# Another order of projections and attention in the three-tile halves of a ragged attention kernel, and other offsets of its code

## The chip, the cores and the metric

The kernel runs on one core of one Trainium2 chip. The metric is device time in microseconds (us) of one execution, the median of several runs; less is better. The engines are named as in the profile: PE is the matrix engine (its weight loads stand apart as PEld), ACT and DVE the two engines that read PSUM, POOL and SP the others; SP and ACT also issue DMAs. L302 is line 302 of the kernel.

## The reference, cut to what matters

For each of 32 batches only the first `seq_len` rows count (lengths between 64 and 511, the same draw each time); everything behind them is zero.

```python
x_b = x[b, :seq_len].copy()                 # seq_len x 512
qkv = np.matmul(x_b, w_qkv)                 # 512 x 1536 weights
q, k, v = np.split(qkv, 3, axis=-1)         # then 8 heads of 64
scores = scale * np.matmul(q, k.transpose(0, 2, 1))
attn = np.exp(scores - scores_max)
attn = attn / (np.sum(attn, axis=-1, keepdims=True) + 1e-08)
out_b = np.matmul(attn, v).transpose(1, 0, 2).reshape(seq_len, dim)
output[b, :seq_len] = out_b
```

## The kernel before, in words

**Pairs and halves.** The batches are sorted by length and taken in 16 pairs. Each pair has a class N (its longer length rounded up to 32, or 340), and T = ceil(N/128) row tiles. A class has its own code. One pair is two halves, h = 0 and h = 1. In a half (`half`, L646) the core does the attention of one batch and, mixed in with it, the projections (Q, K, V from x and the weights) of the next batch, g, whose width is W: N, or the next class's N in the last half of a class. With this draw the pairs are: two with T = 4, six with T = 3 (N = 384, 352, 352, 340, 320, 288), six with T = 2, two with T = 1. The change is about T = 3, the twelve halves in the middle of the run.

**The order is written by hand.** `ORDER[3]` and `DENSE` (L637, L640) are strings of tokens, and `half` turns each token into instructions on PE, ACT and DVE, in that order on each engine. `DENSE` is used where 3N fits in 1024 columns (N = 340, 320, 288), `ORDER[3]` for 384 and 352. The digit i is a pair of heads (0 to 3) or a row tile of V.

- `S` (L304): one key tile's scores for a head pair, two matmuls of N columns on the two halves of PE's rows, then one exp on ACT of 2N columns. Two slots of PSUM, s0 and s1, take turns. A half has twelve.
- `D` (L348): three key tiles at once, eight matmuls into s0 and s1 together, and two exps on ACT of 3N columns. It waits until both slots have been emptied by the exps of the `D` before (L350, L351). A half has four, for head pairs 1, 2, 3 of its own batch and pair 0 of the next one.
- `Q`, `K` (capital letter: emptied from PSUM by DVE, L408; small letter: by ACT, L407): one projection, four matmuls of W columns. `V` (L507): one row tile of V, four matmuls of 512 columns, emptied by DVE (L431).
- `E` then `F`, `G`, `H` or `I` of the same digit, and `U` then `W`: two projections "crossed" (L440, L453). The first token computes with the upper or lower half of the rows, the second finishes with the other half, so that two matmuls always run side by side. The second token waits for the last matmuls of the first (L455). F, G, H, I say which engines empty the Q and the K: DVE/DVE, DVE/ACT, ACT/DVE, ACT/ACT. `W` empties two V tiles by DVE.
- `A` (L511): the weighted sums of one head pair, 18 matmuls of 65 columns, then DVE normalises: a reciprocal (L574) and multiplications into `onat` (L593, L595), two in a half h = 0 and three in a half h = 1. The multiplication of `A1` raises the semaphore `s_of[h][0]`, that of `A3` `s_of[h][1]` (L599).
- `O` (L778): ACT waits for `s_of[h][0]` (L782) and then issues the DMA that stores the first half of the output columns (L1247). As every token, it has a place in ACT's queue: what stands behind it waits with it.

**Banks.** In these halves four PSUM banks (a0, a1, v0, v1) go round (`pick`, L681): a token takes the one that was given back first, or with `~` the second; PE waits until it has been emptied (L278).

**Where the code lies.** For PE the code of a class is cut (`graph`, L1102; `cut`, L70). The block `first` holds the beginning of half 0, up to the last projection that ends within `PIECE` instruction slots. It ends in a branch to `again` (the rest of half 0 and half 1, then back to `first`) if the next pair is of the same class, or to `last` (the same, then on to the next class). `align` (L1116) puts a block at an offset within units of `FETCH` = 256 instructions: `first` at `FIRST[3]`, `again` and with it `last` at `AGAIN`, for dense classes `AT_DENSE`. At the end of a pair that leaves its class PE runs one or two compares, and, where the next class follows at once, a hint and a jump (L1166, L1170, L1121); inside half 0 there is only the branch at the end of `first` (L1207).

## Time and profile before

| | us |
|---|---|
| median of 3 runs | 344.45 (343.46 to 346.18) |
| the profiled execution | 344.15 |
| its span | 342.3 |
| PE busy | 326.2 (95% of the span) |
| ACT busy | 243.5 (71%) |
| DVE busy | 207.8 (61%) |

The span is the part between the first and the last instruction that the profile holds; 1.85 us of that execution lie around it. A row of the timeline has the start in us from the span's start, the duration, engine, line, operation, output and inputs with their shape, the count of merged instructions and, in brackets, how long the engine had been idle before and what ended that. Matmul rows overlap: a matmul's printed end is modelled and includes its way through the array, so what one costs PE is read from start to start. PEq, ACTq and DVEq are the sequencers that hand instructions to their engines.

### The profile page before, as it was taken

The page shows a single profiled execution, that of the slowest core. Times are in us where ns is not written, and L with a number is a line of the kernel's source. Part 1 is how long each engine was busy: PE and PEld are TensorE (multiplying, and loading weights), DVE is VectorE, ACT ScalarE, POOL GpSimd, SP SyncE. Part 2 cuts the span into 40 slices and gives each one's busy share as a digit, 9 for nine tenths or more (in the row PEclk, how much of TensorE's full clock was granted, in tenths as well). Part 3 has the DMA queues.
Part 4 walks back from the last instruction along what each step waited for, and adds up shares of the span by engine and source line. Part 5 has one row for each costly group of instructions (what it writes and reads, how often), then busy time and mean ns, then how long its engine had stood idle before and what let it go on. Part 6 is the DMA issues. An engine that isn't in the chain of part 4 may idle for free. (4 is left out here: it accounts for less than half of the span.)

```text
span 342.3 us, 12067 instructions
## 1 busy us (share of the span) xinstructions
PE 326.2 (95%) x4286; PEld 207.3 (61%) x4287; DVE 207.8 (61%) x548; ACT 243.5 (71%) x349; POOL 63.2 (18%) x102
## 2 busy tenths in 40 slices
PE   6999999999989999999999999999899999999992
PEld 2564554455545555656656657677677776776761
DVE  4676567666654465575556546655666666667672
ACT  4568788777768878878968878878766576566441
POOL 3634020202010110110110111011111121131241
PEclk9999999999999999999999999999999999999998
DMA  6966899666846686885986897997687666778731
GB/s 200 360 196 188 259 372 250 215 198 170 213 156 181 206 274 171 269 292 158 242 305 172 214 307 231 203 255 225 201 157 184 200 183 152 177 180 158 188 106 67
DMA packets 82276, 72.15 MB, mean 211 GB/s; under 512 B 40653, under 2 KB 63181, under 8 KB 82197
## 3 DMA queue, kind: packets, MB, share of 16 engines
q1 hardware_dynamic: 70340, 59.61, 62.9%
q10 hardware_dynamic: 11856, 11.54, 9.8%
q8 instruction: 43, 0.70, 0.9%
q14 instruction: 37, 0.29, 0.3%
HBM read 25.32 MB, written 36.70 MB: 181 GB/s over the span
## 5 line engine op out<-in xcount | busy, mean ns | idle before, releaser
L344 ACT ACTIVATE ep<-psc 128x704 f16<-128x704 f32 (+7 forms) x193 | 156.7, 863 | 57.7 <-PE psc L302 40.9
L302 PE MATMUL pa<-xT,w_r 128*128 128x224 f16 (+20 forms) x996 | 141.8, 276 | 3.0 <-PEq L57 1.7
L302 PEld LDWEIGHTS pa<-xT,w_r 128*128 128x128 f16 (+1 forms) x996 | 76.4, 97 | 38.0 <-issue 17.4
L408 DVE CAST qkT<-pa 128x512 f16<-128x512 f32 (+9 forms) x82 | 47.4, 580 | 45.8 <-PE pa L302 44.5
L302 PE MATMUL pa<-w_r,xT 128*128 128x512 f16 (+3 forms) x360 | 73.4, 348 | 1.6 <-DVE qkT L408 0.9
L302 PE MATMUL psc<-qkT 64*128 64x352 f16 (+17 forms) x702 | 69.4, 287 | 1.3 <-ACT ep L376 0.6
L302 PE MATMUL pav<-v_aug,ep 128*128 128x65 f16 x1468 | 64.2, 194 | 0.0
L302 PEld LDWEIGHTS pav<-v_aug,ep 128*128 128x128 f16 x1468 | 57.4, 98 | 9.2 <-issue 1.6
L1610 POOL CAST v_aug<-masks 128x24 f16 (+4 forms) x33 | 9.1, 276 | 249.4 <-POOLq L1239 249.4
L595 DVE SCALAR_TENSOR_TENSOR onat<-pav,masks,rcp 128x128 f32<-128x128 f32 (+2 forms) x146 | 50.8, 388 | 5.3 <-DVE rcp L574 1.8
L376 ACT ACTIVATE ep<-psc 128x960 f16<-128x960 f32 (+3 forms) x48 | 43.1, 950 | 9.8 <-PE psc L302 8.1
L431 DVE TENSOR_TENSOR v_aug<-pa,masks 128x512 f16<-128x512 f32 (+1 forms) x55 | 37.2, 681 | 18.3 <-PE pa L302 16.2
L302 PEld LDWEIGHTS psc<-qkT 64*128 64x128 f16 x702 | 27.0, 94 | 34.0 <-issue 20.8
L1605 POOL CAST x<-x_nat 128x1536 f16<-128x1536 f32 (+3 forms) x33 | 42.1, 1275 | 9.0 <-POOLq L1239 8.1
L302 PEld LDWEIGHTS pa<-w_r,xT 128*128 128x128 f16 (+1 forms) x360 | 27.3, 96 | 23.2 <-issue 5.2
L407 ACT CAST qkT<-pa 128x320 f16<-128x320 f32 (+7 forms) x70 | 31.0, 460 | 12.4 <-ACTq L57 8.9
L302 PE MATMUL pav<-xT,w_r 64*128 64x352 f16 (+10 forms) x268 | 39.4, 303 | 0.0
L302 PE MATMUL pav<-w_r,xT 64*128 64x512 f16 (+3 forms) x120 | 29.5, 367 | 0.0
L574 DVE RECIPROCAL rcp<-pav 128x8 f32<-128x8 f32 (+1 forms) x74 | 14.7, 199 | 20.3 <-PE pav L302 13.2
L302 PEld LDWEIGHTS pav<-xT,w_r 64*128 64x128 f16 (+1 forms) x268 | 20.3, 95 | 7.7 <-PE pav L302 0.8
L431 DVE TENSOR_TENSOR v_aug<-pav,masks 128x512 f16<-128x512 f32 (+1 forms) x21 | 13.9, 664 | 6.0 <-PE pav L302 5.3
L408 DVE CAST qkT<-pav 128x352 f16<-128x352 f32 (+2 forms) x12 | 6.3, 528 | 17.0 <-PE pav L302 17.0
(77 smaller groups left out, 132.9 us busy)
## 6 DMA issues: line engine op xcount, KB each, us to landing
out_dram<-zt SPq DMA_DIRECT2D x16, 768.0 KB, 5.8
x_nat<-in_x_dram SPq DMA_DIRECT2D x12, 512.0 KB
x_nat<-in_x_dram SPq DMA_DIRECT2D x5, 1024.0 KB
out_dram<-onat ACTq DMA_DIRECT2D x12, 384.0 KB, 4.7
out_dram<-onat SPq DMA_DIRECT2D x12, 384.0 KB, 4.2
x_nat<-in_x_dram SPq DMA_DIRECT2D x17, 256.0 KB, 5.8
out_dram<-onat ACTq DMA_DIRECT2D x16, 256.0 KB, 3.6
x_nat<-in_x_dram SPq DMA_DIRECT2D x4, 768.0 KB
```

The source lines that it names most:

```text
L302: return lambda e: e.matmul(o, lhsT, rhs, start=start, stop=stop)
L344: lambda e: e.activation(out=dst, in_=src, func=AF.Exp, scale=scale),
L376: lambda e, par=par, b=b: e.activation(out=ep[:, i, par, 0:3, 0:N], in_=psc_f[:, par, 0 : 3 * N].rearrange("p (t n) -> p t n", n=N), func= ...
L407: return lambda e: e.copy(out=dst, in_=src)
L408: return lambda e: e.tensor_copy(out=dst, in_=src)
L431: return lambda e: e.tensor_tensor(out=v_aug[h][:, t, lo // HD : lo // HD + n, 0:HD], in0=area[b][:, 0:w].rearrange("p (a d) -> p a d", d=HD),
L574: pr.add("dve", lambda e: e.reciprocal(out=rv, in_=den).then_inc(s_r, 1))
L595: ins = e.scalar_tensor_tensor(scalar=now[0][:, 1, t : t + 1], op0=ALU.mult, op1=ALU.mult, **ops)
L1605: e.tensor_copy(out=x16[h][:, 0:T, :], in_=x_nat[h][:, 0:T, :]).then_inc(s_xc[h], 1)
L1610: e.tensor_copy(out=v_aug[h][:, 0:T, :, HD], in_=src[:, 0, 0:T].unsqueeze(2).broadcast_to([P, T, NH]),).then_inc(s_on[h], 1)
```

## The change

The two strings for T = 3 are written anew. Every token that stands for work is still there; crossed pairs and single ones are chosen differently in the dense string, and some projections are emptied by another engine. Besides, the offsets and the length of the pieces of PE's code change for T = 3.

```diff
-FIRST = {4: 20, 3: 30, 2: 20, 1: None}
-AGAIN = 110
+FIRST = {4: 20, 3: 20, 2: 20, 1: None}
+AGAIN = 2
-AT_DENSE = 0
-PIECE = 222
+AT_DENSE = 20
+PIECE = 257
...
-        3: "U0 S S W0 S E1~ S G1 S E2~ S E0 S I2 S G0 S A0 A1 V2 k3 S S Q3 O A2 A3 S",
+        3: "k3 S S E0 E2~ S F0 S I2 S A0 A1 S U0 S S W0 E1~ S S G1 A2 Q3 O A3 S S V2",
...
-    DENSE = "k3 Q0 k0 D E2~ U0 G2 W0 D q1 A0 k1 A1 D A2 q3~ V2 D O A3"
+    DENSE = "V0 D E1 E2 H1 G2 D A0 q0 O K0~ A1 D V1~ Q3 A2 k3 D A3 V2"
```

In the string for 384 and 352 the halves now end with `S S V2` where they ended with `A2 A3 S`, and begin with the single `k3` where they began with the crossed `U0`. One projection, K0, goes from ACT to DVE. In the dense string the halves end with `A3 V2` and begin with `V0`; the crossed pairs are Q1/K1 and Q2/K2 where they were Q2/K2 and V0/V1; ACT empties four projections where it emptied six. `O` stands before `A1`; it stood behind the last `D`, two tokens of attention after `A1`.

In the code as built (two instructions to a matmul) the block `first` grows from 167 to 215 instructions for 384 and 352, and from 180 to 225 for the dense classes; `last` shrinks from 547 to 500 and from 505 to 460.

## The prediction

> **What bounds the kernel now.** I read the page first, then the busy time by stretch, then PE's waits in the stretch of T = 3, then the timeline at the places that the change moves.

> ```profile
> PE 326.2 (95%) x4286; PEld 207.3 (61%) x4287; DVE 207.8 (61%) x548; ACT 243.5 (71%) x349; POOL 63.2 (18%) x102
> ```
> ```profile
> 98.80:125.30 26.50, 24.95 (x345) 14.69 (x344) 13.70 (x39) 20.45 (x34) 3.40 (x4) 1.00 0.70 209
> 125.30:174.40 49.10, 48.27 (x690) 29.86 (x688) 28.55 (x89) 40.05 (x68) 6.80 (x8) 1.00 0.80 243
> 174.40:243.40 69.00, 67.46 (x984) 46.74 (x982) 40.55 (x129) 55.12 (x84) 10.21 (x12) 1.00 0.80 224
> ```
> ```profile
> PE pa L302 <- PEq L57: 1.9, 5, 0.5
> PE pa L302 <- DVE qkT L408: 0.9, 1, 0.9
> PE pa L302 <- issue: 0.7, 1, 0.7
> PE psc L302 <- ACT ep L376: 0.6, 2, 0.3
> PE psc L302 <- PEq L57: 0.3, 1, 0.3
> ```

> The three stretches are the pair of N = 384, the two of 352, and the three dense ones; columns are length, then busy us of PE, PEld, DVE, ACT, POOL, clock, DMA share, GB/s. PE is busy 140.7 of 144.6 us, at clock 1.00, and PE's own waits there come to 4.4 us. So PE's queue sets the end; the amount of matrix work does not change, and what can be won is waits, which the last five rows name: five starts of a pair (PEq), the entry from T = 4 (DVE), one gap inside a half (issue), the exit to T = 2 (ACT, and one PEq). ACT, 55.1 of 69 us in the dense stretch, has little slack there: it can become the bound.

> **Part 1: the start of a pair.**

> ```profile
> 121.44 1.03 PE L302 MATMUL pav<-w_r,xT 128*128 128x512 f16 x4
> 122.31 0.76 PE L302 MATMUL pa<-xT,w_r 128*128 128x352 f16 x4
> 123.00 0.47 PE L302 MATMUL psc<-qkT 64*128 64x352 f16 x4
> 123.41 0.77 PE L302 MATMUL pa<-xT,w_r 128*128 128x352 f16 x4
> 124.02 1.26 PE L302 MATMUL pav<-v_aug,ep 128*128 128x65 f16 x36
> 125.21 0.32 PE L302 MATMUL psc<-qkT 64*128 64x352 f16 x2
> 125.99 1.04 PE L302 MATMUL pa<-w_r,xT 64*128 64x512 f16 x8 [0.46 <-PEq L57]
> 126.85 0.48 PE L302 MATMUL psc<-qkT 64*128 64x352 f16 x4
> 127.15 1.04 PE L302 MATMUL pa<-w_r,xT 64*128 64x512 f16 x8
> ```

> Four score matmuls take 127.15 - 126.85 = 0.30 us, so two take 0.15; after the last `S` of the pair (125.21) PE could go on at 125.36 and goes on at 125.99. The loss is 0.63, of which the row prints 0.46. Five such starts lose 1.9 + 5 x 0.17 = 2.75 us. In that time PE's sequencer goes through the branches. After the change a `V` stands last, 122.31 - 121.44 = 0.87 us long and only eight instructions, behind two `S` (0.30). The sequencer hands them over early and branches meanwhile; the loss of 0.63 lies under 0.87. In the two dense starts only `A3` (0.55) and `V` lie ahead, and the `D` before them may start late (part 3), so I leave 0.1 each: **-2.5 us**. If the cover fails, all of it stays.

> **Part 2: the entry, the exit, the gap, the switches.**

> ```profile
> 98.51 0.68 DVE L431 TENSOR_TENSOR v_aug<-pa,masks 128x512 f16<-128x512 f32 x1
> 99.11 0.58 DVE L408 CAST qkT<-pa 128x416 f16<-128x416 f32 x1
> ```
> ```profile
> 99.83 1.04 PE L302 MATMUL pa<-w_r,xT 64*128 64x512 f16 x8 [0.89 <-DVE qkT L408]
> 111.09 0.68 PE L302 MATMUL pa<-v_aug,ep 128*128 128x65 f16 x17
> 112.44 0.19 PE L302 MATMUL pa<-v_aug,ep 128*128 128x65 f16 x1 [0.67 <-issue]
> ```
> ```profile
> 243.85 0.39 PE L302 MATMUL psc<-qkT 64*128 64x256 f16 x4 [0.32 <-ACT ep L376]
> ```

> Entry: `U0` needs a0 and a1, and a1 is emptied at 99.11 + 0.58 = 99.69, 0.14 before it starts. `k3` needs a0 alone, emptied at 98.51 + 0.68 = 99.19, so it starts near 99.33, and `E0`, which needs a1, comes a microsecond later: **-0.5**. Next late is nothing: two free slots wait for the `S`.

> Exit: the first scores of T = 2 wait for the exps of the last `D`, 0.32 before the first of them, and about as much before the next. Now `V2` stands between, there 256 columns wide, half of 0.87: **-0.4**. In that half, too, `U0` crossed a V of 512 columns with one of 256 at the wide one's pace, 2 x 0.86 (125.99 to 126.85); singly they are 0.87 + 0.43: **-0.4**.

> The gap: the row of 17 `A2` matmuls and the one after a hole of 0.67. Counted from the branch to `last`, it is matmul 72, instruction 144. The block begins at offset 110 of 256: the boundary comes after 146. So I read it as code that had not arrived. With offset 2 the boundary comes after 254, in half 1, twice as long after the branch: **-0.7**, between 0 and -0.8 (start to start).

> Switches: four projection matmuls followed by a score take 123.00 - 122.31 = 0.69, followed by `A` 124.02 - 123.41 = 0.61. A change between full and half rows costs 0.08. The string for 384 and 352 has six a half where it had four (+1.0 in six halves), but `G1` comes two scores after `E1` and no longer one, which gives about 0.1 back, as do smaller bubbles: **+0.2**, between 0 and +1. The dense string has six before and after.

> **Part 3: `O` ahead of `A1`, in six dense halves.**

> ```profile
> 182.35 0.71 PE L302 MATMUL pav<-v_aug,ep 128*128 128x65 f16 x18
> 182.99 0.61 PE L302 MATMUL psc<-qkT 64*128 64x340 f16 x8
> 183.54 0.72 PE L302 MATMUL pa<-v_aug,ep 128*128 128x65 f16 x18
> 184.09 0.74 PE L302 MATMUL pa<-xT,w_r 128*128 128x340 f16 x4
> 184.67 1.03 PE L302 MATMUL pav<-w_r,xT 128*128 128x512 f16 x4
> 185.71 0.61 PE L302 MATMUL psc<-qkT 64*128 64x340 f16 x8
> ```
> ```profile
> 183.10 0.20 DVE L574 RECIPROCAL rcp<-pav 128x6 f32<-128x6 f32 x1 [0.21 <-PE pav L302]
> 183.64 1.93 ACT L376 ACTIVATE ep<-psc 128x1020 f16<-128x1020 f32 x2 [0.29 <-PE psc L302]
> 183.67 0.34 DVE L595 SCALAR_TENSOR_TENSOR onat<-pav,masks,rcp 128x128 f32<-128x128 f32 x1
> 187.13 0.38 ACTq L1247 DMA_DIRECT2D out_dram<-onat  x1
> ```
> ```profile
> 194.78 0.18 DVE L574 RECIPROCAL rcp<-pav 128x6 f32<-128x6 f32 x1
> 195.00 0.87 DVE L595 SCALAR_TENSOR_TENSOR onat<-pav,masks,rcp 128x128 f32<-128x128 f32 x3
> ```
> ```profile
> 335.30 0.75 DVE L595 SCALAR_TENSOR_TENSOR onat<-pav,masks,rcp 128x512 f32<-128x512 f32 x1 [0.25 <-DVEq L57]
> 336.30 0.56 ACTq L789 DMA_DIRECT2D out_dram<-onat  x1
> 337.08 0.60 ACT L344 ACTIVATE ep<-psc 128x512 f16<-128x512 f32 x1 [1.55 <-ACTq L57]
> ```

> The first two fences are one half 0 of N = 340. `A1` starts at 182.35, the third `D` at 182.99, its exps run 183.64 to 185.57, and the fourth `D` starts 0.14 later, at 185.71: it is the exps that hold it, by some 0.1. So from exps to next `D` is 2.07.

> After the change ACT's queue reads: exps of the second `D`, copy of Q0, wait for `A1`'s sums, DMA, exps of the third `D`. `A1` is normalised at 183.67 + 0.34 = 184.01, 1.66 after it starts. The place where ACT waits for such a store today is T = 1: normalised at 335.30 + 0.75 = 336.05, next exp at 337.08, 1.03 later, 0.56 of it the DMA. With the DMA of T = 3 (0.38) that is 0.85; the T = 1 store also raises a second semaphore, so I take 0.8. The third exps start 1.66 + 0.8 = 2.46 after `A1` starts, 1.82 after their `D` (today 0.65), and the fourth `D` can start 1.82 + 2.07 = 3.89 after the third. Meanwhile PE has that `D` (0.55 with a switch), `V1` (0.87), `Q3` (0.58), `A2` (0.55), `k3` with a switch (0.66): 3.21. PE waits **0.68**. In a half 1 DVE multiplies three times: 194.78 to 195.87 is 1.09 where half 0 has 0.91, so the exps come 0.18 later; with narrower next projections PE has 3.14 and waits 0.95. By the same sum, with matmuls and exps in proportion to their columns, the six halves wait 0.68, 0.95, 0.67, 0.99, 0.66 and 1.42 (in the last, V, Q and K are 256 wide), 5.4 us. Today the fourth `D`s wait some 0.6 in all, the PEq row of 0.3 among them: **+4.8**. From below, the DMA alone (0.38) behind sums that had long been there would cost nothing, since 183.64 + 0.38 is still within what `V1` adds; from above, 0.85 and 1.0 instead of 0.8 makes +5.1 to +6.

> **Part 4: the crossed pairs.** Between the first two `D` lie four tokens of 8 half-row matmuls, now all W wide, where two were 512 wide. At 0.86 for 512, 340 columns take 0.57 (an estimate), four of them 2.28; with the `D` 2.73. From `D` to its exps 0.65, from exps to `D` 2.07: 2.72. For 340 it just fits; for a narrower next batch it does not: by proportion 0, 0.13, 0.05, 0.25, 0.12 and 0.32, **+0.9**. In return the waits swallow small bubbles of today's dense halves: **-0.3**. Of the emptying that goes from ACT to DVE I count nothing: DVE is busy 40.6 of 69.0 us there, and every bank comes round again more than a token later.

> **Sum.** -2.5 - 0.5 - 0.4 - 0.4 - 0.7 + 0.2 + 4.8 + 0.9 - 0.3 = +1.1 us on the profiled execution of 344.15 (span 342.3 and 1.85 around it): 345.25, taken as **345.2**. The median of the runs shown, 344.45, is 0.3 above that execution, so I forecast about 0.2% over it: no change that a measurement of this kernel can tell, which takes about 1%. What is won at the pair starts, the dense halves give back.

> **The rivals.**

> *Faster: `O` does not hold the exps.* If the sums of `A1` were there 1.2 us sooner (1.82 less today's 0.65), part 3 falls away: 345.2 - 4.8 = 340.4. Against it: the token's place in ACT's queue and the T = 1 rows. For it: I have no row of T = 3 in which ACT waits like this. Chance 0.12.

> *Slower: code arrives late in every pair.* The first pieces grow to 215 and 225 instructions from offset 20, so they end at 235 and 245 of 256, and the jump then needs the next unit at once. If a hole as at 112.44 opened at each of these six branches, it would cost 6 x 0.7 and the 0.7 credited would be lost: 345.2 + 4.9 = 350.1. It decides the matter from three of the six on (348.0). Against it: eleven pieces out of twelve run today without a hole of that kind (issue: 0.7, once), and the jump has a hint ahead of it. Chance 0.09.

> ```profile
> q8 instruction: 43, 0.70, 0.9%
> ```

> 43 packets carried 0.70 MB, 16 KB each. [...]

> *The change does not do what it says: pair starts stay.* If the sequencer hands `V2` over so late that its branches do not fit under it, the 2.5 us stay: 347.7. For it: it must first get past the late `D`. Against it: eight instructions of 0.87 us. Chance 0.10.

> **How the numbers follow.** The forecast as summed has 0.62, with a range of its own of 343.5 to 346.8 (0.7 of the gap, 1 of the switches, 1 of the store either way); 0.07 is left for what I do not see. The range for 8 in 10, 342.4 to 347.9, reaches to the case of the starts and leaves out most of the other two rivals. Faster by over 1% (below 341.0) has the first rival and little else: 0.09. Slower by over 1% (above 347.9) has the second and half of the third: 0.13. Within 1%: 0.78.

> **What would show it.** Right: no PEq row above 0.1 at the starts of T = 3; first matmul of 384 near 99.3; in each dense half ACT idle up to the third exps, about 1.8 after their `D`, and a gap on PE of 0.6 to 1.4 ahead of the fourth `D`, named ACT. Wrong: exps 0.65 after the third `D` (first rival), new gaps named issue near the branches (second), PEq rows kept (third).

## The result, and the profile after

The changed kernel takes 346.88 us (median of 6 runs, 346.75 to 347.64) against 344.44 (343.46 to 346.18): a ratio of 1.0073, with a 95% interval from 1.0047 to 1.0099. Measured once more in a later session, beside new runs of the kernel before, it was 1.0071 (1.0043 to 1.0098). So it is 0.7% slower, within the 1% that the prediction calls no change. Ratios and intervals are worked out from the undisturbed executions alone and medians and ranges from all, so that two medians need not divide to the ratio beside them. The changed kernel's profiled execution took 346.75, with a span of 344.6.

The busy time by stretch, cut at the same places of the work as the prediction's first fence (the pair of 384, the two of 352, the three dense ones), and the matmul engine's waits from the entry to the exit of T = 3:

```profile
PE 325.7 (95%) x4286; PEld 206.4 (60%) x4287; DVE 215.9 (63%) x566; ACT 238.4 (69%) x331; POOL 63.1 (18%) x102
```
```profile
99.89:125.19 25.30, 25.00 (x345) 14.73 (x345) 15.16 (x45) 20.48 (x33) 3.40 (x4) 1.00 0.83 235
125.19:173.17 47.98, 47.98 (x690) 29.43 (x689) 30.21 (x93) 39.73 (x65) 6.80 (x8) 1.00 0.79 249
173.17:245.50 72.33, 67.37 (x983) 46.24 (x981) 44.70 (x137) 50.85 (x73) 10.20 (x12) 1.00 0.76 215
```
```profile
PE psc L302 <- PEq L57: 3.1, 3, 1.3
PE psc L302 <- ACT ep L376: 2.0, 4, 0.8
PE pa L302 <- DVE v_aug L431: 0.3, 1, 0.3
```

The first pair went from 26.50 to 25.30, the second stretch from 49.10 to 47.98 and has not a single wait left (PE 47.98 of 47.98). The dense stretch went from 69.00 to 72.33. The five starts on projections (`pa`) and the hole are gone from the list; in their place stand seven waits on scores (`psc`), six of them the fourth `D`s and one the exit. Three carry the name PEq: there the sequencer passed the semaphore last, but the row ahead of it on ACT is late (below); ACT had been idle for 1.95, 2.02 and 2.07 before the third exps of these halves.

From the first matmul of T = 3 to the first projection of T = 2 it takes 146.18 (100.33 to 246.51), where it took 145.04 (99.83 to 244.88); second profiles of both kernels gave 146.26 and 145.00. The entry wait, which lies ahead of that, fell from 1.05 to 0.46 start to start. So the part that the prediction works on cost 0.55, and the medians differ by 2.4. Some 0.35 of the rest lies outside the span: 2.1 to 2.3 us of every execution of the changed kernel, 1.7 to 1.9 of the kernel before. All trials below that have both new strings show the former, all others the latter; why is open. What then remains is taken up below.

Start of the first pair of 352 in the timeline, to be held against the rows at 125.21 and 125.99 of before:

```profile
123.91 0.47 PE L302 MATMUL psc<-qkT 64*128 64x352 f16 x4
124.32 1.04 PE L302 MATMUL pav<-w_r,xT 128*128 128x512 f16 x4
125.19 0.76 PE L302 MATMUL pa<-xT,w_r 128*128 128x352 f16 x4
125.88 0.47 PE L302 MATMUL psc<-qkT 64*128 64x352 f16 x4
```

`V2` at 124.32 and `k3` at 125.19 are 0.87 apart, which is V2's own length: nothing is lost. Entry and exit:

```profile
100.33 0.82 PE L302 MATMUL pa<-xT,w_r 128*128 128x384 f16 x4 [0.30 <-DVE v_aug L431]
...
246.18 0.39 PE L302 MATMUL psc<-qkT 64*128 64x256 f16 x4 [0.24 <-ACT ep L376]
```

And the first dense half, to be held against the rows from 182.35 to 185.71 of before; ACT's and DVE's rows of the same moments follow it:

```profile
179.17 0.71 PE L302 MATMUL pav<-v_aug,ep 128*128 128x65 f16 x18
179.82 0.61 PE L302 MATMUL psc<-qkT 64*128 64x340 f16 x8
180.36 1.04 PE L302 MATMUL pav<-w_r,xT 128*128 128x512 f16 x4
...
182.36 0.74 PE L302 MATMUL pav<-xT,w_r 128*128 128x340 f16 x4
183.58 0.61 PE L302 MATMUL psc<-qkT 64*128 64x340 f16 x8 [0.48 <-ACT ep L376]
```
```profile
181.07 0.38 ACTq L1247 DMA_DIRECT2D out_dram<-onat  x1
181.50 1.93 ACT L376 ACTIVATE ep<-psc 128x1020 f16<-128x1020 f32 x2 [1.58 <-ACTq L57]
```
```profile
180.49 0.34 DVE L595 SCALAR_TENSOR_TENSOR onat<-pav,masks,rcp 128x128 f32<-128x128 f32 x1
```

`A1` starts at 179.17 and is normalised at 180.49 + 0.34 = 180.83, 1.66 later, as before. ACT then issues the store (181.07) and starts the third exps at 181.50, 1.68 after their `D` (179.82); it was 0.65. The fourth `D` comes at 183.58. `Q3` alone would have let it go at 182.36 + 0.58 = 182.94, so 0.64 is lost.

### The profile page after: what moved, and what is told of

It is laid out like the page before. It is cut to its first block, busy times and chain, and to the rows that moved or that the text cites. A ratio compares the mean times of both kernels' runs of the same rounds, so it can differ in the third digit from the quotient of the medians.

```text
span 344.6 us, 12070 instructions
## 1 busy us (share of the span) xinstructions
PE 325.7 (95%) x4286; PEld 206.4 (60%) x4287; DVE 215.9 (63%) x566; ACT 238.4 (69%) x331; POOL 63.1 (18%) x102
## 5 line engine op out<-in xcount | busy, mean ns | idle before, releaser
L344 ACT ACTIVATE ep<-psc 128x704 f16<-128x704 f32 (+7 forms) x193 | 156.8, 858 | 58.6 <-PE psc L302 40.9
L302 PE MATMUL pa<-xT,w_r 128*128 128x224 f16 (+21 forms) x972 | 133.1, 276 | 4.1 <-PEq L57 1.7
L302 PEld LDWEIGHTS pa<-xT,w_r 128*128 128x128 f16 (+1 forms) x972 | 73.6, 97 | 37.3 <-issue 14.8
L302 PE MATMUL pa<-w_r,xT 128*128 128x512 f16 (+3 forms) x360 | 72.9, 348 | 0.0
L302 PE MATMUL psc<-qkT 64*128 64x352 f16 (+17 forms) x702 | 67.0, 287 | 5.3 <-PEq L57 3.1
L408 DVE CAST qkT<-pa 128x512 f16<-128x512 f32 (+9 forms) x82 | 47.3, 578 | 35.3 <-PE pa L302 34.3
L302 PE MATMUL pav<-v_aug,ep 128*128 128x65 f16 x1414 | 62.2, 194 | 0.0
L302 PEld LDWEIGHTS pav<-v_aug,ep 128*128 128x128 f16 x1414 | 55.1, 98 | 9.7 <-issue 1.2
L376 ACT ACTIVATE ep<-psc 128x960 f16<-128x960 f32 (+3 forms) x48 | 43.1, 949 | 20.8 <-ACTq L57 13.1
L431 DVE TENSOR_TENSOR v_aug<-pa,masks 128x512 f16<-128x512 f32 (+1 forms) x61 | 41.3, 682 | 18.0 <-PE pa L302 17.4
L595 DVE SCALAR_TENSOR_TENSOR onat<-pav,masks,rcp 128x128 f32<-128x128 f32 (+2 forms) x137 | 48.2, 391 | 5.6 <-DVE rcp L574 2.1
L302 PEld LDWEIGHTS psc<-qkT 64*128 64x128 f16 x702 | 26.0, 94 | 34.9 <-issue 24.2
L302 PE MATMUL pav<-xT,w_r 64*128 64x352 f16 (+11 forms) x340 | 46.2, 300 | 0.0
L302 PEld LDWEIGHTS pa<-w_r,xT 128*128 128x128 f16 (+1 forms) x360 | 27.2, 97 | 24.2 <-issue 4.7
L407 ACT CAST qkT<-pa 128x352 f16<-128x352 f32 (+7 forms) x58 | 26.3, 458 | 12.8 <-ACTq L57 6.3
L574 DVE RECIPROCAL rcp<-pav 128x8 f32<-128x8 f32 (+1 forms) x71 | 14.1, 199 | 28.5 <-PE pav L302 18.8
L302 PEld LDWEIGHTS pav<-xT,w_r 64*128 64x128 f16 (+1 forms) x340 | 24.7, 95 | 8.6 <-issue 1.1
L408 DVE CAST qkT<-pav 128x352 f16<-128x352 f32 (+5 forms) x30 | 14.8, 501 | 16.6 <-PE pav L302 15.9
L302 PE MATMUL pav<-w_r,xT 128*128 128x512 f16 (+2 forms) x72 | 17.7, 367 | 0.0
L302 PEld LDWEIGHTS pa<-v_aug,ep 128*128 128x128 f16 x378 | 13.4, 98 | 3.7 <-issue 2.2
```

Of the source, the lines that this page charges most:

```text
L302: return lambda e: e.matmul(o, lhsT, rhs, start=start, stop=stop)
L344: lambda e: e.activation(out=dst, in_=src, func=AF.Exp, scale=scale),
L376: lambda e, par=par, b=b: e.activation(out=ep[:, i, par, 0:3, 0:N], in_=psc_f[:, par, 0 : 3 * N].rearrange("p (t n) -> p t n", n=N), func= ...
L407: return lambda e: e.copy(out=dst, in_=src)
L408: return lambda e: e.tensor_copy(out=dst, in_=src)
L431: return lambda e: e.tensor_tensor(out=v_aug[h][:, t, lo // HD : lo // HD + n, 0:HD], in0=area[b][:, 0:w].rearrange("p (a d) -> p a d", d=HD),
```

## The experiments

All twelve were timed beside fresh runs of the kernel before, whose medians were 344.76 to 345.54 in these sessions; ratios are to those. "T = 3" below is the time from its first matmul to the first projection of T = 2.

**The store behind the last D** (of the changed kernel; `-` is the changed kernel, `+` the trial):

```
-    DENSE = "V0 D E1 E2 H1 G2 D A0 q0 O K0~ A1 D V1~ Q3 A2 k3 D A3 V2"
+    DENSE = "V0 D E1 E2 H1 G2 D A0 q0 K0~ A1 D V1~ Q3 A2 k3 D O A3 V2"
```

> The changed kernel with one token of the dense string moved: O stands behind the last D again, and no longer ahead of A1. Theory (the store holds the third exps): the six waits ahead of the fourth D (0.64, 1.01, 0.67, 1.09, 0.97, 1.48 in the changed kernel, 5.9 in all) fall to about 0.1 each, the third exps start some 0.65 after their D, and the time falls by 5.3, from 346.9 to 341.6 (340.8 to 342.6), below both kernels. Rival (the wide crossed pair and the copies that went to other engines hold the fourth D, the store only happens to stand there): the waits stay within a few tenths and the time stays near 346.9. In between, near 344, both have a share.

342.70 (341.0 to 343.8), ratio 0.9917 (0.9886 to 0.9948); T = 3 took 142.85. All six fourth `D`s lose 0.1, the switch alone: the 5.9 are down to 0.6. T = 3 fell by 3.3 and not by 5.3, because smaller waits came up in other places (0.52, 0.53, 0.44 and 0.44 start to start), the two longest at a crossed token:

```profile
188.12 0.72 PE L302 MATMUL pa<-xT,w_r 64*128 64x320 f16 x8 [0.34 <-PEq L57]
```
```profile
L1074 PEldq TENSOR_LOAD <-cls x16: 297/421/1022, 47.2 to 332.5; - x16
```

The second row groups the loads of the next class into a register by the matmul engine's sequencer (shortest, median, longest in ns). One of them, 0.95 long, stands just ahead of 188.12, one of 1.02 ahead of the other. A load took between 0.30 and 1.02 here, and in two halves a long one showed at a crossed token. Why their length varies is open.

**The store early in the kernel before:**

```
-    DENSE = "k3 Q0 k0 D E2~ U0 G2 W0 D q1 A0 k1 A1 D A2 q3~ V2 D O A3"
+    DENSE = "k3 Q0 k0 D E2~ U0 G2 W0 D q1 A0 k1 O A1 D A2 q3~ V2 D A3"
```

> The kernel before with one token of the dense string moved: O ahead of A1, nothing else. Theory: the third exps wait for the normalised sums of A1 and the DMA, start 1.8 after their D as in the changed kernel, and the fourth D could start 1.82 + 2.07 = 3.89 after the third, where today 2.72 pass: a wait of about 1.2 in half 0 of N = 340 and up to 1.4 in others, some 7 in all, so 351 (349.5 to 352.5). That the wait is longer than in the changed kernel is part of the theory: between the third and fourth D the old string has one token less of half-row work. Rival (the store is harmless, the other moves of the dense string cost the time): 344.4, within 0.5.

354.03 (351.9 to 354.6), ratio 1.0232 (1.0185 to 1.0278). One token does it, in the old string as well:

```profile
183.30 0.61 PE L302 MATMUL psc<-qkT 64*128 64x340 f16 x8
...
187.06 0.61 PE L302 MATMUL psc<-qkT 64*128 64x340 f16 x8 [1.06 <-ACT ep L376]
```
```profile
184.56 0.38 ACTq L1247 DMA_DIRECT2D out_dram<-onat  x1
184.98 1.93 ACT L376 ACTIVATE ep<-psc 128x1020 f16<-128x1020 f32 x2 [1.33 <-ACTq L57]
```

The third exps start 184.98 - 183.30 = 1.68 after their `D`, as in the changed kernel, and the fourth `D` 3.76 after the third, in both. The six waits are 1.22, 1.46, 1.18, 1.53, 1.12 and 1.97, 8.5 in all, so 7.2 more than the 1.3 of before. The expectation had "some 7"; T = 3 grew by 9.3, and part of the other 2 is a lower clock behind these waits (a mean of 0.75 from 203 to 208, last section).

**The store behind the third D** (of the changed kernel):

```
+    DENSE = "V0 D E1 E2 H1 G2 D A0 q0 K0~ A1 D O V1~ Q3 A2 k3 D A3 V2"
```

> The changed kernel with O one step later in the dense string: right behind the third D (and its exps on ACT), no longer ahead of A1. Theory (what counts is only that the store stands ahead of the third exps in ACT's queue): the six waits ahead of the fourth D go as they did with O behind the last D (0.1 each, the switch), 342.7 (341.5 to 344). The sums of A1 are normalised some 1.0 after the third exps start, and these last 1.9, so ACT has nothing to wait for there. Rival (a store in the middle of the half costs its issue of 0.38 in any place): the fourth exps come 0.4 later and each half keeps 0.3 to 0.4, 345.

342.26 (340.9 to 343.5), ratio 0.9923 (0.9890 to 0.9955); T = 3 took 141.32, the shortest of all. ACT's rows of the same half:

```profile
181.08 1.02 ACT L376 ACTIVATE ep<-psc 128x1020 f16<-128x1020 f32 x1 [0.54 <-PE psc L302]
181.80 0.38 ACTq L1247 DMA_DIRECT2D out_dram<-onat  x1
182.00 1.01 ACT L376 ACTIVATE ep<-psc 128x1020 f16<-128x1020 f32 x1
```

The store is now issued at 181.80, while the first of the two exps runs, and the second follows at 182.00, 0.92 after the first; the pair elsewhere keeps that distance too (1.93 for both, of which the second takes 1.01). So the 0.38 itself cost nothing here, where the sums were ready under an exp; what cost was ACT standing still for them (1.58 idle ahead of the third exps in the changed kernel, 0.29 in the kernel before).

**The long string alone, and the dense one alone.** The first is the changed kernel with the old `DENSE`; the second is the kernel before with the new `DENSE`, `AT_DENSE = 20` and `PIECE = 257`.

> One half of the change: the new string of N = 384 and 352 and the new code places, with the old dense string. Theory (the long string gains, the dense one loses): three pair starts gone (0.64, 0.46, 0.53), the entry 0.6 shorter, the hole of 0.8 gone, four more switches and smaller bubbles for about +0.2 in all: 3 us less than the kernel before, 341.4 by its median of 344.4 (340.4 to 342.6), with the two starts between dense pairs (0.6 and 0.5) still there. Rival (the old dense string does not fit the new places, as the old long string did not): a jump of 2 us or more at one of the dense starts, 345 or more.

> The other half of the change: the new dense string at its new place (20, pieces up to 257), with the old string of N = 384 and 352 at its old places (30 and 110). Theory: the stretch of the dense pairs takes 73.4 instead of 69.7 us, as in the changed kernel, the rest as before: 348.1 (347 to 349), and with the part of the long string (3 less) it adds up to the change. Rival (the two parts meet: the waits of the dense halves are there because the pairs ahead of them are faster): 345 or less.

The long string: 343.01 (340.7 to 344.6), ratio 0.9913 (0.9884 to 0.9943), T = 3 in 142.96, 2.1 less, and the entry 0.6 less. The dense string: 349.06 (347.7 to 349.5), ratio 1.0089 (1.0057 to 1.0122), T = 3 in 148.72, 3.7 more. Against that stand 0.6 less and 1.1 more for the change as a whole. The two trials' 1.6 is 0.5 more, and one wait is as long: in the second a register load of 1.03, as above, stands ahead of a crossed token at 192.53, which starts 0.49 late; the changed kernel has no such wait. Both times lie just above their ranges: against the 345.54 of their session the long string gains 2.5, where 3 was expected. One gain and one loss, each in its own place; the waits of the dense halves (0.64 to 1.54) don't depend on the pairs ahead of them.

**V not last:**

```
-        3: "k3 S S E0 E2~ S F0 S I2 S A0 A1 S U0 S S W0 E1~ S S G1 A2 Q3 O A3 S S V2",
+        3: "k3 S S E0 E2~ S F0 S I2 S A0 A1 S U0 S S W0 E1~ S S G1 A2 Q3 O A3 V2 S S",
```

> The changed kernel with the end of its long string turned: V2 S S instead of S S V2, so that the last V stands ahead of the last two scores and no longer covers the branches. Same work, same lengths of code. Theory (a V at the end hides the sequencer's branches): the starts after the pairs of 384, 352 and 352 lose about 0.6 each again, named PEq, and the time rises by 1.5 to 1.9, to 348.6. Rival (the starts went because the next pair begins with k3, which needs one bank and not two, or because of the code places): no start reappears, 346.9.

351.05 (349.8 to 352.2), ratio 1.0158 (1.0123 to 1.0192): slower than expected, and for another reason. No start lost anything; the V, one token earlier, covered the branches as well (at the first start `k3` comes 0.41 after the `S S`, as the projection behind the four scores at 123.00 does in the rows of before). The loss comes two tokens later:

```profile
112.03 0.77 PE L302 MATMUL pa<-xT,w_r 128*128 128x352 f16 x4
112.85 0.34 PE L302 MATMUL psc<-qkT 64*128 64x384 f16 x2
113.55 0.34 PE L302 MATMUL psc<-qkT 64*128 64x384 f16 x2 [0.37 <-ACT ep L344]
```

`S S k3 S S` are four scores with one short token among them, and the exps are not done with the first two. So this trial didn't decide what it was made for. It showed that the V at the end also parts the scores.

**A3 last in both strings:**

```
-    ... G1 A2 Q3 O A3 S S V2          ... k3 D A3 V2
+    ... G1 V2 A2 Q3 O S S A3          ... k3 D V2 A3
```

> The changed kernel with A3 at the end of both strings and V2 earlier: ... G1 V2 A2 Q3 O S S A3 in the long one, D V2 A3 in the dense one. The next pair still begins with k3 or V0. Theory (the sequencer's branches need a token of few, long instructions ahead of them; A3 has 36 short ones in 0.55): the five starts lose 0.4 to 0.6 each again, 2.5 in all, named PEq, and the time rises to 349.3 (348.2 to 350.2). Rival (the starts went because the next pair begins with a single projection): no start reappears, 346.9.

350.01 (348.9 to 352.3), ratio 1.0164 (1.0122 to 1.0205). The PEq starts are back, all five:

```profile
PE pa L302 <- PEq L57: 2.1, 5, 0.5
```

Start to start they lose 0.67, 0.42, 0.70, 0.69 and 0.43, 2.9 in all; T = 3 took 149.34, 3.2 more than in the changed kernel. The next pair begins with its single projection as before, so that is not what hides the branches: the long token ahead is.

**The places.** Three trials change where the pieces of code lie: the new strings at the old places (30, 110, 0, 222), the old strings at the new ones (20, 2, 20, 257), and the changed kernel with `AGAIN = 110` alone.

> The strings of the changed kernel at the code places of the kernel before (30, 110, 0, pieces up to 222). Theory (the strings make the time, the places are worth the one hole of 0.7 at most): 346.9, between 346.2 and 348; the work ahead of T = 3 and behind it takes what it takes in the changed kernel. Rival (the places are what costs the 1.1 us by which the changed kernel reaches T = 4 later and the 0.7 that it loses behind T = 3): 345.1 or, with the hole back, 345.8, and the first projection of T = 4 starts near 15.5 and not 16.6.

> The strings of the kernel before at the code places of the changed kernel (20, 2, 20, pieces up to 257). Theory: only the hole of 0.7 in the first 352 half goes (start to start 0.8), the pair starts keep their 2.7: 343.7 (343.2 to 344.6). Rival (the places bring the 1.1 ahead of T = 3 and the 0.7 behind it): 345.5. Third: a boundary falls on another matmul and the hole is only moved: 344.4.

> The changed kernel with one place changed: the second pieces of N = 384 and 352 begin at 110 of 256 again and not at 2, all else as in the changed kernel. Theory (the last piece of a pair must not cross into a new unit of 256 instructions shortly before it jumps: the new half has about 497 instructions, from 2 it ends at 499, from 110 at 607, 95 past the boundary at 512): the jumps after the pairs of 384, 352 and 352 wait, as in the run of the new strings at the old places, 1.5, 1.5 and 3.7, and the time rises by about 6.7 to 353.6 (350 to 356). Rival (it was the lengths of the first pieces, cut at 222, that cost there): 346.9.

They took 356.09 (353.2 to 360.5), 361.44 (359.3 to 366.2) and 355.26 (350.4 to 356.6), ratios 1.0290 (1.0221 to 1.0358), 1.0444 (1.0390 to 1.0499) and 1.0229 (1.0168 to 1.0291). None of the theories for the first two had this; the third's had the time, but not which starts are late. Line 1121 is in `align`, which puts a jump ahead of a block that is to begin at its offset; at the end of a pair that jump leads on to the next pair's first piece. Here it is in the changed kernel, with the old strings at the new places, and with `AGAIN` alone (shortest, median, longest in ns), and the longest start of the last two:

```profile
L1121 PEldq COMPARE_BRANCH  x13: 206/313/413, 25.1 to 312.2; - x13
```
```profile
L1121 PEldq COMPARE_BRANCH  x13: 196/315/5842, 24.3 to 327.8; - x13
```
```profile
L1121 PEldq COMPARE_BRANCH  x13: 206/313/3859, 24.0 to 317.7; - x13
```
```profile
131.24 1.89 PE L302 MATMUL pa<-w_r,xT 64*128 64x512 f16 x8 [6.09 <-PEq L57]
```
```profile
127.56 1.09 PE L302 MATMUL pa<-xT,w_r 128*128 128x352 f16 x4 [3.13 <-PEq L57]
```

In time the jump takes 0.3, late it takes 2.2 to 5.8. It was late after the pairs of 384, 352 and 352 in the first two trials, after the first and the third of them in the last (start to start 3.3 and 1.5).

```profile
q8 instruction: 1, 0.02, 1.0%
```

The hole of the kernel before is of the same kind: a packet landed at 110.94, and the matmul at 112.44 came 1.50 later. The three other profiles with that hole have 1.48 to 1.61. From the steady distance I read these stalls as waits for code. Why a packet comes late is not shown; in that longest stall the DMA engines were moving data at the same time (a share of 0.84 from 125.0 to 131.2).

Nor does a rule for the places come out of this. `AGAIN` alone shows that the place of the second pieces makes the jumps late. By the count of the trace, the code from `AGAIN` to the end of the half is some 545 instructions in the old string and 497 in the new one. So the pair's last boundary of 256 lies 143 instructions ahead of the end in the kernel before (110 + 545 = 655), and none is near in the changed one (2 + 497 = 499); both are in time. It lies 35 ahead with the old string at 2, and 95 ahead with the new one at 110, and there jumps are late. That the distance of this boundary decides is a reading that fits the long pairs, but for the one start that was spared, from 352 to 352. It doesn't fit the dense ones: the old dense string at 20, in the second trial and in the long string alone, ends at 20 + 505 = 525, 13 behind a boundary, and its jumps took 0.31 to 0.34.

**The kernel before once more:**

> The kernel before once more, with a profile of its own, as the measure of scatter. Theory (what the profiles show outside T = 3 is scatter): a ratio of 1.000 within 0.3%, T = 3 again 144.9 from its first matmul to the first projection of T = 2, and the stretch behind it anywhere between 97.3 and 99.5, since the first transposes of T = 1 took between 2.9 and 5.4 in the runs so far. Rival (the 97.6 behind T = 3 belong to the old long string, whose four profiles so far have 97.3 to 99.0, where the nine with the new one have 97.9 to 100.8): again below 98.2, with transposes of less than 3.8.

345.95 (343.8 to 348.3), ratio 1.0019 (0.9990 to 1.0047). T = 3 took 145.00, as the theory had it, and the stretch behind it 97.5 with a transpose of 3.0, as the rival had it. This and the second run of the changed kernel were for the rest of the 2.4:

> The changed kernel itself once more, beside fresh runs of the kernel before. Theory (only what happens from the entry of T = 3 to its exit belongs to the change, 0.5 to 0.6 more; the 1.1 ahead of T = 3 and 0.7 behind it in the first profile are scatter of loads): a ratio of 1.000 to 1.005, T = 4 beginning anywhere between 15.4 and 17.1, and T = 3 again taking 146.0 from its first matmul to the first of T = 2. Rival (these 1.8 belong to the changed kernel): a ratio of 1.006 to 1.009, and T = 4 beginning near 16.6.

The ratio of 1.0071 is the rival's, but T = 4 did not begin near 16.6. Ahead of T = 3 the matter is settled. The changed kernel reached the long projections of T = 4 at 16.59 in its first profile and at 15.41 in the second, the kernel before at 15.51 and 16.27: scatter. Behind T = 3 it does not look like scatter alone. The last stretch, T = 1, of the kernel before, twice, and of the changed one, twice:

```profile
321.30:342.30 21.00, 14.02 (x244) 10.18 (x244) 10.47 (x21) 6.86 (x11) 5.48 (x12) 0.94 0.34 105
```
```profile
322.10:342.90 20.80, 13.98 (x244) 10.11 (x244) 10.42 (x21) 6.81 (x11) 5.41 (x12) 0.93 0.30 95
```
```profile
323.30:344.60 21.30, 13.85 (x244) 10.12 (x244) 10.51 (x21) 6.88 (x11) 5.47 (x12) 0.90 0.34 103
```
```profile
321.80:344.70 22.90, 13.90 (x244) 10.12 (x244) 10.52 (x21) 6.89 (x11) 5.44 (x12) 0.94 0.37 98
```

The same 244 matmuls take 21.0 and 20.8, and 21.3 and 22.9. In the longest of the four:

```profile
323.44 1.23 SPq L1458 DMA_TRANSPOSE xT<-x  x1
...
328.27 0.61 POOL L1653 COPY xT<-xT 128x512 f16<-128x512 f16 x1 [3.00 <-POOLq L1239]
329.02 1.18 PE L302 MATMUL pa<-xT,w_r 128*128 128x96 f16 x24 [1.68 <-PEq L57]
```

SP issues the transpose of the next pair's input at 323.44, POOL copies it at 328.27, and PE, which was ready, starts at 329.02. From issue to copy it is 4.8 there, 3.5 in the changed kernel's other profile, 3.7 and 3.0 in the two of the kernel before. Over all fourteen profiles, what lies behind T = 3 takes 97.1 to 98.6 with the old long string (five) and 97.8 to 100.7 with the new one (nine), counted from the first projection of T = 2 (the expectations count from the sequencer's entry, 0.2 earlier). The two sets overlap. The changed kernel's two profiles lose 0.6 and 2 there; in the second it is an input that arrives late, in the first, with its 3.5, it isn't. Neither loss was tried, and the cause of both stays open.

## Why the prediction was right

The forecast of 345.2 lies 1.7 below the measured 346.88, inside its range, and the sum of its terms for T = 3, +1.1, stands against +0.55 measured (1.14 inside, less 0.59 at the entry).

- **Part 1, the starts, -2.5: right.** All five are gone, with 2.75 of loss; the 0.1 left for the late `D`s was not needed. With `A3` last all five came back (2.9), so the cover is the long V. The wait ahead of the fourth `D` did not upset it.
- **Part 2: right.** Entry -0.59 for -0.5; the hole is gone (0.82 for 0.7; that a boundary of 256 made it was an estimate from the count, instruction 144 with the boundary after 146, and no run shows it); the two first scores of T = 2 wait 0.5 where they waited 0.95, -0.43 for -0.4. The two stretches of long pairs give back 1.20 and 1.12, where entry and hole make 1.41 and two starts 1.09, so that about 0.2 is left for the switches and bubbles, as forecast. In the exit half `U0` and `W0` took 1.64 by the rows from 234.91 to 237.89 of before, and two single `V` take 1.31: -0.33 for -0.4.
- **Part 3, the store, +4.8: right in mechanism and size.** The six waits are 0.64, 1.01, 0.67, 1.09, 0.97 and 1.48, 5.9 in all, where 0.68, 0.95, 0.67, 0.99, 0.66 and 1.42 were forecast; less the 1.3 that the fourth `D`s of before lose start to start (the forecast took 0.6), that is +4.6. The exps start 0.67 behind the sums, between the DMA alone (0.38) and the 0.8 taken. What was too low is the fifth, 0.66 for 0.97. Moving `O` alone, in either kernel, moved these waits and the time with them.
- **Part 4, the crossed pairs, +0.9: wrong in place, too big.** No second `D` waits. The loss falls on the crossed tokens themselves, 0.10 to 0.24 in four of the six halves, about 0.4 more in all than before.
- **The rival "O does not hold the exps"** fell with the rows at 181.07 and 181.50, and with the trials that move it.
- **The rival "code arrives late in every pair"** did not happen: the branches at the ends of the first pieces (L1207), where it looked for the holes, took 0.07 to 0.45 in T = 3 in every run. Late code there was, with either string at the other's places, but at the jump to the next pair, which the rival did not name, and at 1.5 to 6 a jump and not at 0.7. Four numbers beside the strings decide between 0.7% and 2.9% slower, and the profile of before had only the hole of 0.7 to price that by.
- **The rival "pair starts stay"** fell: no PEq row is left at a start.
- **What no step had:** the 0.6 to 2 behind T = 3 and the 0.35 outside the span. The prediction counted nothing there. Of the 2.4 between the medians T = 3 makes 0.55 and the time outside the span 0.35; the other 1.5 is of the size of the loss behind T = 3. So the forecast came out right for the stretch that it works on; that its range also took in what it did not see was luck.

The experiments give three versions below both kernels: the new long string with the old dense one (343.01), and the changed kernel with `O` behind the last `D` (342.70) or behind the third (342.26). All are 0.8 to 0.9% under the kernel before and cannot be told apart.

## What to carry to other kernels

A wait in ACT's queue was paid here by what stood behind it (the third exps started 1.68 after their `D` with the store ahead of them, 0.65 without): put a store behind work that lasts until its data are ready, not ahead of work that could run at once. The sequencer's branches were hidden here by few, long instructions ahead of them: the eight of a `V`, 0.87, did it, and the 76 of two `A` and an `S`, 1.34, lost 0.63. When a string of code changes length, try its places again (either string at the other's places made it 2.9% and 4.4% slower than the kernel before), and look at the last code packet ahead of each jump: here the eight jumps whose packet landed 0.7 to 4.5 after they had begun were late, and none of those at the ends of T = 3's pairs whose packet had landed 1.47 or more ahead was.

## What was not expected of the hardware

A long stall of the matmul engine was paid twice here. Behind the start that came 6.09 late, and behind the one of 3.13, the granted clock (third figure from the right) was 0.74 in the stretch that follows; last, the same work in the kernel before, at 1.00:

```profile
131.20:140.00 8.80, 8.76 (x80) 4.58 (x82) 1.82 (x3) 5.55 (x9) 1.76 (x2) 0.74 0.43 106
```
```profile
127.50:134.00 6.50, 6.45 (x75) 3.71 (x76) 1.08 (x3) 4.09 (x8) 1.76 (x2) 0.74 0.31 62
```
```profile
126.00:134.80 8.80, 8.72 (x121) 5.17 (x122) 4.15 (x13) 8.03 (x14) 1.70 (x2) 1.00 0.69 202
```

In 8.80 us PE did 80 matmuls and not 121. The clock was not a little lower all along: it was 0.50 from 128 to 131 behind the second of these starts, and 1.00 from 131.3 on. Ahead of the first row lay 6.09 of idle time, ahead of the second 3.13. A third case had less: in the kernel before with its store early no single wait was over 2.0, yet the mean clock from 203 to 208 was 0.75, behind waits of 1.46 and 0.70 that lay 1.8 apart. So here shorter waits close together came ahead of it. In the changed kernel, with waits of 0.6 to 1.5 some 12 apart, the clock stayed at 1.00 throughout T = 3. What decides when it falls is not shown.
